# The first three activation blocks of a two-layer decoder trunk, loaded from ScalarE's DMA queue instead of SyncE's

## The chip, the cores and the metric

The kernel runs on one core of one Trainium2 chip. A core has five engines, each with its own instruction stream that is worked off strictly in the order in which it was written into the program: PE (TensorE, matmuls), DVE (VectorE), ACT (ScalarE), POOL (GpSimd) and SP (SyncE, which here only starts DMAs). An engine that meets a wait holds up everything behind it in its own stream. The metric is the device time of one execution in microseconds (us), the median over several runs. Lower is better.

## What is computed

The reference is the forward pass of a decoder trunk of two layers over 256 positions (`S`) of width 2048 (`D`), in float32. Layer 0 mixes dilated sliding-window attention (8 heads) with gated linear attention (GLA, 4 heads); layer 1 mixes an S5 state-space block with HGRN2 heads. Both have one combined input projection, a SiLU gate and one output projection. Cut to what the change touches, which is the very beginning:

```python
def rmsnorm(x, g):
    xf = x.astype(jnp.float32)
    return xf * lax.rsqrt(jnp.mean(xf * xf, axis=-1, keepdims=True) + EPS) * g

def ab_layer(h, w_in, gla_w_gate, gla_b_gate, gla_norm_g, w_out):
    z = h @ w_in                               # h: 256 x 2048, the normalised x
    qa, ka, va, qb, kb, vb, g_low, gate = jnp.split(z, AB_SPLIT, axis=-1)
    ...
    return y @ w_out

h = x
h = h + ab_layer(rmsnorm(h, norm_g[0]), ...)   # layer 0
h = h + cd_layer(rmsnorm(h, norm_g[1]), ...)   # layer 1
out = rmsnorm(h, final_g)
```

## The kernel before

**Tiling.** The activations lie transposed in SBUF: 16 blocks of 128 channels by 256 positions (`kt` = 0 to 15). They share one tile `xv` (L75) with a table of 220 small vectors (`NV`), which stands in its first columns. Every projection is a chain of blocks of 512 output columns. For one block the weights stream in as four groups `g` of four `kt` each, 1 MB a group, into one of three buffers `raw` (L144). A float32 product is built from three products of rounded parts: ACT rounds a weight half group into `wh` (L168), DVE puts what is left into `wl` (L169), and PE adds `wh·xh + wh·xl + wl·xh`, where `xh` and `xl` are the same two parts of the activations, made once by `split_x` (L204 to L206). `gemm_fm` (L174) gives the result with channels on the partitions, 12 matmuls of 256 columns for each `kt` (L181); `gemm_tm` (L193) gives it with positions on the partitions, 6 matmuls of 512 columns for each `kt` (L200). `wh` and `wl` have three buffers each, and one buffer holds two `kt`, so that ACT and DVE can work at most three half groups ahead of PE.

**The first projection.** The very first block (`psq`, L241, the q of GLA) can start only when the first activations and weights have come. For it `load_split` cuts both into smaller pieces. In group 0 each `kt` is loaded alone: first its piece of `xv`, then its weights, and the weights of `kt` 0 in two halves. The piece of `kt` 0 carries the table of vectors with it (476 columns in place of 256). Groups 1 to 3 come in halves of two `kt`. All these loads go through `load` (L229), which starts them on SP's queue and chains each behind the last with `tc.issue_after`, so that SP's order is as written.

**What sets the order.** The program is written with a tile framework that schedules the instructions itself, by a timeline that it estimates while it builds the program (`schedule_with_timeline_sim=True`, L1126). `urgent()` (L72) raises the priority of what stands in it. So the order in which an engine meets its instructions is not that of the source, and an edit at one place can move instructions at others, wherever the estimate of one time tips the choice.

**What comes behind, and is spoken of below.** While the first two projections run, ACT and DVE also square and sum the activations (`square_sum`, L105 to L111, with a single scratch tile `gf`, L109) and DVE works out the S5 parameters (`s5_prep`, L807 to L932, some 150 small operations). When the first projection is done, ACT evacuates it from PSUM into `gq` (L390). The second projection gives k (`gk`, L359), the third and fourth give v by `gemm_tm`. In between PE turns two small S5 matrices `co` round (L937), ACT copies them out (`et`, L938), POOL stores them to DRAM (`ed`, L940) and loads them again spread over the partitions (`E`, L953), and DVE multiplies with them (L976 to L981). GLA's own small matmuls (L287, 32 of 32x32 for each of its levels) are strewn between the projections' matmuls. Much later, around 650 us, ACT sends S5 results `ys` to DRAM (L638), gets them back as `yc` and works on them (L643).

Of the kernel before, what the change touches and what calls it, by code (L numbers as in the profile page):

```python
# [57 lines left out]
def trunk(ctx: ExitStack, tc: tile.TileContext, I, out):  # L58
    nc = tc.nc
# [12 lines left out]
    def urgent():  # L72
        return tc.high_priority(offset=HI)

    xv = const.tile([128, NV + KT * S], F32, name="xv")  # L75
# [59 lines left out]
    def hook():  # L135
        if fillq:
            todo = fillq.pop(0)
            if todo:
                with tc.issue_after(state["mm"].ins):
                    for fn in todo:  # L140
                        fn()

    def load_split(src, g):
        raw = stream.tile([128, 4, 512], F32, name="raw", bufs=3)  # L144
        first = state["first"]
        state["first"] = first and g < 3
        with urgent():
            if first:
                for a, b in ((0, 1), (1, 2), (2, 3), (3, 4)) if g == 0 else ((0, 2), (2, 4)):
                    xs = slice(NV + (4 * g + a) * S if g + a else 0, NV + (4 * g + b) * S)  # L150
                    load(xv[:, xs], I["xv"][:, xs])
                    for c in (slice(0, 256), slice(256, 512)) if g + a == 0 else (slice(0, 512),):
                        load(raw[:, a:b, c], src[g][:, a:b, c])
                for kt in range(4 * g, 4 * g + 4):
                    split_x(kt, V_NG0)
            else:
                state["load"] = nc.sync.dma_start(raw, src[g])
        if first and g == 3:
            load_consts()
        for half in range(2):  # L160
            wh = stream.tile([128, 2, 512], F32R, name="wh", bufs=3)
            wl = stream.tile([128, 2, 512], F32R, name="wl", bufs=3)
            with urgent():
                for a, b, c, d in (((0, 1, 0, 256), (0, 1, 256, 512), (1, 2, 0, 512)) if first and g == 0
                                   else ((0, 2, 0, 512),)):
                    r = raw[:, 2 * half + a:2 * half + b, c:d]
                    w, l = wh[:, a:b, c:d], wl[:, a:b, c:d]
                    state["wh"] = A.activation(w, r, AF.Copy)  # L168
                    V.tensor_sub(l, r, w)  # L169
            for k in range(2):  # L170
                yield 4 * g + 2 * half + k, wh[:, k], wl[:, k]
            hook()
# [13 lines left out]
    def _iter(src, groups, mid, order):  # L186
        for n, g in enumerate(order or range(groups)):
            for m, (kt, wh, wl) in enumerate(load_split(src, g)):
                yield 4 * n + m, kt, wh, wl
            if mid and 2 * (n + 1) == groups:  # L190
                mid()
# [12 lines left out]
    def split_x(kt, go):  # L204
        A.activation(xh[:, kt], hT[:, kt], AF.Copy, scale=col(go + kt))
        V.scalar_tensor_tensor(xl[:, kt], hT[:, kt], col(go + kt), xh[:, kt], op0=OP.mult, op1=OP.subtract)  # L206
# [15 lines left out]
    def load_consts():  # L222
        nc.sync.dma_start(cst, I["cst"])
        nc.sync.dma_start(glw, I["w_low"])
        for n in range(2):
            nc.sync.dma_start(wgt[16 * n:16 * n + 16], I["w_gate"])
        nc.sync.dma_start(msk.rearrange("p a b -> p (a b)"), I["msk"])

    def load(dst, src):  # L229
        prev = state.get("load")  # L230
        with tc.issue_after(prev.ins) if prev else ExitStack():
            state["load"] = nc.sync.dma_start(dst, src)
# [906 lines left out]
```

## Time and profile before

| | us |
|---|---|
| median of 3 runs | 888.54 (887.33 to 891.26) |
| profiled execution, whole | 894.61 |
| its span, first to last instruction | 892.7 |
| DVE busy | 636.0 (71%) |
| ACT busy | 473.1 (53%) |
| POOL busy | 54.4 (6%) |

The profile is of one execution of its own; its 894.61 us lie 6.07 us above the median of the runs, and 1.9 us of it lie outside the span. A row of the timeline reads: start in us, duration in us, engine, source line, operation, tile written `<-` tiles read, form, count, and in brackets the time for which the engine sat idle before it and what ended that. Rows of the same kind are merged, and a duration then runs to the end of the last. Durations of neighbours overlap, since an engine begins an instruction before the last is quite through, so that spacing is read from the starts. `ACTq`, `SPq` rows are the issue of a DMA on that engine's queue. A row of the windows reads: stretch, its length, busy time and instructions of PE, weight load, DVE, ACT and POOL, then the granted clock of PE, the mean busy share of the 16 DMA engines, and GB/s.

### The profile page before, as it was taken

Reading aid. Unit: us, or ns where it says so; the run is one execution under the profiler, and the core shown is the slowest. Engines: PE = TensorE matmul, PEld = TensorE weight load, DVE = VectorE, ACT = ScalarE, POOL = GpSimd, SP = SyncE. Lnnn points to the kernel's source line nnn. Section 1 sums busy time; section 2 is a strip of 40 time slices with the busy share of each in tenths; the row PEclk is TensorE's granted clock in tenths of the full one; section 3 lists DMA queues with packets and bytes.
Section 4 is the critical chain, followed back from the end, with each engine's and each line's share of the span. In section 5 each row is a group of like instructions: output and inputs, shape, how many; then the busy total and the mean of one; then the engine's idle time right before and its main releaser. Section 6 shows DMA issues by size and latency. Waiting matters only on the chain.

```text
span 892.7 us, 18688 instructions
## 1 busy us (share of the span) xinstructions
PE 874.1 (98%) x7728; PEld 804.5 (90%) x7728; DVE 636.0 (71%) x1197; ACT 473.1 (53%) x715; POOL 54.4 (6%) x106
## 2 busy tenths in 40 slices
PE   8999999999999999999999999999999999999995
PEld 8987899888998899999999999899867899988894
DVE  7987975888869868755575586877977655665562
ACT  7654546665655765644443345455545475444451
POOL 0001100111101101000000001100110000000000
PEclk9999999999999999999999999999999999999998
DMA  9827744777756655555575766754654455544432
GB/s 316 318 99 217 257 159 146 231 253 217 264 193 220 223 179 182 206 189 189 190 270 195 267 211 227 247 192 166 222 170 160 183 189 189 189 171 179 176 136 94
DMA packets 40388, 180.40 MB, mean 202 GB/s; under 512 B 12720, under 2 KB 14256, under 8 KB 22768
## 3 DMA queue, kind: packets, MB, share of 16 engines
q1 hardware_dynamic: 29440, 154.99, 49.5%
q0 software_dynamic: 7984, 22.69, 7.7%
q10 hardware_dynamic: 2880, 1.54, 0.6%
q8 instruction: 60, 0.98, 0.4%
q14 instruction: 24, 0.20, 0.1%
HBM read 166.48 MB, written 12.71 MB: 201 GB/s over the span
## 4 chain that ended last, share of the span: by engine, by line
PE 74%; DVE 8%; ACT 6%; DMA 5%; issue 5%; SPq 0%; POOL 0%; POOLq 0%; DVEq 0%; ACTq 0%
PE pg L181 48%; PE pg L200 17%; DVE wl L169 2%; PE pg L758 2%; DMA tabs<-pc 2%; ACT wh L168 1%; PE pm L287 1%; DMA E<-ed 1%; PE pm L339 1%; DMA s5y<-ys 1%; ACT bb L1021 1%; DMA raw<-in_w_dram 1%; ACT x L1039 1%; PE pm L308 1%; DVE PP L1005 1%
## 5 line engine op out<-in xcount | busy, mean ns | idle before, releaser
L168 ACT ACTIVATE wh<-raw 128x1024 fp32r<-128x1024 f32 (+2 forms) x276 | 287.6, 1046 | 325.0 <-PE pg L181 187.6
L169 DVE TENSOR_TENSOR wl<-raw,wh 128x1024 fp32r<-128x1024 f32 (+2 forms) x276 | 332.6, 1207 | 173.7 <-ACT wh L168 165.0
L181 PE MATMUL pg<-xh,wh 128*128 128x256 f32 x1024 | 162.8, 281 | 1.8 <-ACT wh L168 1.7
L181 PE MATMUL pg<-xl,wh 128*128 128x256 f32 x1024 | 163.8, 280 | 0.0
L181 PE MATMUL pg<-xh,wl 128*128 128x256 f32 x1024 | 163.4, 281 | 0.1
L181 PEld LDWEIGHTS pg<-xh,wh 128*128 128x128 f32 x1024 | 137.4, 188 | 3.7 <-ACT wh L168 3.1
L181 PEld LDWEIGHTS pg<-xl,wh 128*128 128x128 f32 x1024 | 138.0, 188 | 0.8 <-issue 0.3
L181 PEld LDWEIGHTS pg<-xh,wl 128*128 128x128 f32 x1024 | 137.9, 189 | 0.8 <-DVE wl L169 0.3
L200 PE MATMUL pg<-wh,xh 128*128 128x512 f32 x320 | 100.4, 395 | 1.8 <-ACT wh L168 1.8
L200 PE MATMUL pg<-wl,xh 128*128 128x512 f32 x320 | 101.0, 396 | 0.5 <-DVE wl L169 0.4
L200 PE MATMUL pg<-wh,xl 128*128 128x512 f32 x320 | 101.0, 395 | 0.0
L200 PEld LDWEIGHTS pg<-wh,xh 128*128 128x128 f32 x320 | 59.3, 188 | 14.8 <-ACT wh L168 2.2
L200 PEld LDWEIGHTS pg<-wl,xh 128*128 128x128 f32 x320 | 59.5, 188 | 14.1 <-DVE wl L169 1.3
L200 PEld LDWEIGHTS pg<-wh,xl 128*128 128x128 f32 x320 | 59.9, 188 | 12.8
L181 PE MATMUL pg<-yh,wh 128*128 128x256 f32 x320 | 50.8, 281 | 0.0
L181 PE MATMUL pg<-yl,wh 128*128 128x256 f32 x320 | 50.6, 281 | 0.0
L181 PE MATMUL pg<-yh,wl 128*128 128x256 f32 x320 | 50.6, 281 | 0.0
L181 PEld LDWEIGHTS pg<-yl,wh 128*128 128x128 f32 x320 | 43.4, 190 | 0.1
L181 PEld LDWEIGHTS pg<-yh,wh 128*128 128x128 f32 x320 | 43.2, 189 | 0.1
L181 PEld LDWEIGHTS pg<-yh,wl 128*128 128x128 f32 x320 | 43.1, 189 | 0.0
L967 POOL DMA_DIRECT2D tabs<-pc x44 | 23.8, 546 | 167.0 <-DVE x L977 43.7
L200 PE MATMUL pg<-wh,yh 128*128 128x512 f32 x96 | 30.1, 394 | 0.0
(350 smaller groups left out, 994.0 us busy)
## 6 DMA issues: line engine op xcount, KB each, us to landing
raw<-in_w_dram SPq DMA_DIRECT2D x100, 1024.0 KB, 5.0
raw<-in_wo_dram SPq DMA_DIRECT2D x28, 1024.0 KB, 4.8
tb<-tabs POOLq DMA_DIRECT2D x8, 768.0 KB, 6.4
tabs<-pc POOLq DMA_DIRECT2D x20, 256.0 KB, 5.7
raw<-in_wg_dram SPq DMA_DIRECT2D x4, 1024.0 KB, 4.8
raw<-in_wo1l_dram SPq DMA_DIRECT2D x4, 1024.0 KB, 4.8
raw<-in_w_dram SPq DMA_DIRECT2D x6, 512.0 KB, 7.4
tabs<-pc POOLq DMA_DIRECT2D x24, 128.0 KB, 4.9
```

Of the source, the lines that this page charges most:

```text
L168: state["wh"] = A.activation(w, r, AF.Copy)
L169: V.tensor_sub(l, r, w)
L181: state["mm"] = T.matmul(ps[:, c], w[:, cs], a[:, kt], start=(i == 0 and n == 0 and c % 2 == 0), stop=(i == last and n == 2), skip_group_c ...
L200: state["mm"] = T.matmul(ps[:, t], a[:, kt, ts_], w, start=(i == 0 and n == 0), stop=(i == last and n == 2), skip_group_check=True)
L287: T.matmul(ps[32 * b:32 * b + 32, t, hd], k[:, hd, r], Q[:, hd, r], start=True, stop=True)
L308: T.matmul(ps[j0:j0 + h, hd, j0 + h:j0 + 2 * h], k[:, hd, b:b + h], Qp[:, hd, b + h:b + 2 * h], start=True, stop=True)
L339: T.matmul(ps[:, (hd - h0) * dv:(hd - h0 + 1) * dv], AT[:, hd, t + j], v[:, j, hd * dv:(hd + 1) * dv], start=(j == 0), stop=(j == t))
L758: T.matmul(ps[:, t, 0:256], a_[:, kt, ts_], w_, start=(kt == 0 and n == 0), stop=(kt == KT - 1 and n == 2), skip_group_check=True)
L967: nc.gpsimd.dma_start(tabs[qt, dst, n], t[src].rearrange("p a b -> p (a b)"))
L1005: V.scalar_tensor_tensor(PP[half[1 - g], g].rearrange("p a b c -> p (a b c)"), x1[half[g]], -1.0, x2[half[g]], op0=OP.mult, op1=OP.subtract)
L1021: A.activation(bb[half[g ^ n], g], z[n][half[g]].unsqueeze(2).to_broadcast([64, 8, 4, 16]), AF.Copy)
L1039: A.activation(v8(x1)[:, r_], cst[:, C_ID64:C_ID64 + 64], AF.Copy, scale=vec[:, V_D + 8 * qt + r_:V_D + 8 * qt + r_ + 1])
```

## The change

```diff
@@ -148,7 +148,10 @@
             if first:
                 for a, b in ((0, 1), (1, 2), (2, 3), (3, 4)) if g == 0 else ((0, 2), (2, 4)):
                     xs = slice(NV + (4 * g + a) * S if g + a else 0, NV + (4 * g + b) * S)
-                    load(xv[:, xs], I["xv"][:, xs])
+                    if g == 0 and a < 3:
+                        nc.scalar.dma_start(xv[:, xs], I["xv"][:, xs])
+                    else:
+                        load(xv[:, xs], I["xv"][:, xs])
                     for c in (slice(0, 256), slice(256, 512)) if g + a == 0 else (slice(0, 512),):
                         load(raw[:, a:b, c], src[g][:, a:b, c])
```

The pieces of `xv` for `kt` 0, 1 and 2 are started on ACT's queue. They stand outside the chain of `load`; the weights stay on SP and stay chained. Nothing else is written differently, but the scheduler gives other orders on PE, DVE, ACT and SP: in the first 120 us of the program, and again at the last S5 quarter around 650 us. In between they agree but for a few DMA issues on SP, and POOL's order is the same throughout. In the listings below the changed kernel's line numbers are 3 higher from L155 on (L171 is L168 of before); the text uses the numbers of before.

The start of ACT's stream before, from its first instruction on (`wact` is a dummy that brings the table load forward, `ge` a small exponential):

```order
L235 ACT_TABLE_LOAD
L235 ACTIVATE wact<-ones 128x1
L205 ACTIVATE xh<-xv 128x256
L168 ACTIVATE wh<-raw 128x256
L258 ACTIVATE ge<-ge 128x16
L168 ACTIVATE wh<-raw 128x256
```

The same place in the changed kernel:

```order
L152 DMA xv<-in_xv_dram 128x476
L152 DMA xv<-in_xv_dram 128x256
L171 ACT_TABLE_LOAD
L171 ACTIVATE wh<-raw 128x256
L152 DMA xv<-in_xv_dram 128x256
L208 ACTIVATE xh<-xv 128x256
L171 ACTIVATE wh<-raw 128x256
```

Two of the loads stand ahead of the table load, the third behind the first rounding of weights, which waits for its data.

ACT at the end of the first projection, before. The first row makes the last `wh` of the first projection, and the two rows of `wh` ahead of `gq` (which evacuates that projection) are the first two of the second projection:

```order
L168 ACTIVATE wh<-raw 128x1024
L107 ACTIVATE sqa<-xv 128x1024
L110 ACTIVATE gf<-xv 128x1024
L368 ACTIVATE glhl<-glw 128x16x16
L110 ACTIVATE gf<-xv 128x1024
L168 ACTIVATE wh<-raw 128x1024 x2
L390 ACTIVATE gq<-pg 128x1024
L110 ACTIVATE gf<-xv 128x1024
L168 ACTIVATE wh<-raw 128x1024 x7
```

The same place in the changed kernel:

```order
L171 ACTIVATE wh<-raw 128x1024
L107 ACTIVATE sqa<-xv 128x1024
L110 ACTIVATE gf<-xv 128x1024
L371 ACTIVATE glhl<-glw 128x16x16
L110 ACTIVATE gf<-xv 128x1024
L393 ACTIVATE gq<-pg 128x1024
L110 ACTIVATE gf<-xv 128x1024
L171 ACTIVATE wh<-raw 128x1024 x8
```

The first two `wh` of the second projection have moved behind the evacuation `gq` and the third squaring `gf`. On DVE the third addition L111 has likewise moved ahead of the second projection's first `wl`.

DVE where the S5 parameters meet their reloaded matrices `E`, before. The `wl` ahead of L976 is the eleventh of the third and fourth projections (v), and the one behind L979 the twelfth:

```order
L169 TENSOR_TENSOR wl<-raw,wh 128x1024
L891 TENSOR_TENSOR up_717<-up_717,tmp 128x32
L976 TENSOR_TENSOR pc<-E,pB 128x512
L977 TENSOR_TENSOR x_1593<-E,pB 128x512
L978 TENSOR_TENSOR pc<-E,pB 128x512
L979 TENSOR_TENSOR x_1594<-E,pB 128x512
L169 TENSOR_TENSOR wl<-raw,wh 128x1024
```

In the changed kernel the `wl` ahead is the fifth of these projections, and the one behind is the sixth:

```order
L172 TENSOR_TENSOR wl<-raw,wh 128x1024
L894 TENSOR_TENSOR up_689<-up_689,tmp 128x32
L330 TENSOR_TENSOR gT_1401<-gT_1363 128x128
L979 TENSOR_TENSOR pc<-E,pB 128x512
L980 TENSOR_TENSOR x_1593<-E,pB 128x512
L981 TENSOR_TENSOR pc<-E,pB 128x512
L982 TENSOR_TENSOR x_1594<-E,pB 128x512
L890 TENSOR_TENSOR tmp<-up_689 128x32
L892 TENSOR_TENSOR up_696<-up_689 128x32
L330 TENSOR_TENSOR gT_1439<-gT_1401 128x64
L172 TENSOR_TENSOR wl<-raw,wh 128x1024
```

The four multiplications that need `E` stand six half groups of weights earlier. What makes `E` has moved as well. PE's two transposes L937 stand before the 53rd and the 61st matmul of v in the old order, and 20 and 11 matmuls before the end of the second projection in the new one; the matmuls L379 that lead to GLA's decay stand 30 matmuls earlier. Of GLA's small matmuls L287, the first two sets of 32 stand in 6 places of PE's old order up to the end of v (5, 1, 4, 3, 2 and 17+32) and in 12 places of the new one.

## The prediction

> **What bounds the kernel now.** I read the page first, then PE's busy time by stretches, then the timeline wherever PE idles or the change moves something.
>
> ```profile
> span 892.7 us, 18688 instructions
> ...
> 0.00:10.00 10.00, 7.72 (x44) 6.85 (x45) 5.20 (x30) 5.71 (x13) 1.76 (x7) 1.00 0.76 225
> ...
> 100.00:150.00 50.00, 48.89 (x731) 45.78 (x730) 35.35 (x57) 27.31 (x51) 2.12 (x4) 1.00 0.54 191
> ...
> 600.00:700.00 100.00, 97.96 (x1162) 84.16 (x1161) 78.36 (x126) 54.23 (x89) 7.38 (x13) 1.00 0.52 180
> ```
>
> PE is the bound. Outside the first 10 us (2.28 us idle), a 1.11 us gap near 117 us and 2.04 us near 650 us it hardly stops before the tail. So what makes PE idle is paid at the end in full, whatever the other engines save.
>
> **The first loads.** Removed from SP: three issues. Added to ACT: three issues, two ahead of the table load, one behind the first `wh`.
>
> ```profile
> 0.73 0.38 SPq L232 DMA_DIRECT2D xv<-in_xv_dram  x1
> 1.17 0.90 SPq L232 DMA_DIRECT2D raw<-in_w_dram  x2
> 0.73 1.28 ACT L235 ACT_TABLE_LOAD   x1 [0.73 <-PEq L1122]
> ...
> 2.00:3.00 1.00, 1.00 (x6) 1.00 (x6) 0.00 (x0) 0.21 (x2) 0.29 (x2) 1.00 0.88 293
> 3.00:4.00 1.00, 1.00 (x7) 1.00 (x5) 0.63 (x8) 0.63 (x2) 0.00 (x0) 1.00 0.66 168
> 4.00:5.00 1.00, 0.81 (x4) 0.34 (x3) 1.00 (x6) 0.38 (x2) 0.00 (x0) 1.00 0.95 296
> 5.00:6.00 1.00, 0.44 (x3) 0.44 (x4) 0.49 (x4) 0.89 (x2) 0.00 (x0) 1.00 0.75 203
> ...
> 12.79 0.73 PE L181 MATMUL pg<-xh,wh 128*128 128x256 f32 x4 [0.53 <-ACT wh L168]
> ```
>
> An issue takes SP about 0.45 us, so the weights can start 0.45 us earlier at once and 1.35 us earlier after the third. But the DMA engines were already 0.88, 0.66, 0.95 and 0.75 busy between 2 and 6 us; what a denser queue can fill there is 0.12 + 0.34 + 0.05 + 0.25 = 0.76 us, and PE's last start-up wait (12.79) hangs on that stream. Against it, ACT issues until 1.65 us and loads its table until 2.93; the first `xv` shares the engines with weights that used to come after it; the third piece waits behind `wh`. I take a gain of 0.6 us (between 1.1 and a loss of 0.5).
>
> The Trainium skill ("DMA: Bandwidth & Descriptors", Issuing engines are not separate DMA queues) says that all queues run on the same 16 engines and a second one saves only issue time; by that rule the gain would be the issue time, up to 1.35 us, and the busy shares above agree that little more than that is there to win. The Trainium skill ("ScalarE: Activation LUTs", What ACT_TABLE_LOAD costs) gives 1.28 us for the load and 1.38 for a drain; by it `wh` would start a little over 1 us later and the gain become a small loss, but the row above is followed by an activation at 2.02, with no drain to be seen.
>
> **Second projection: a new stall.** ACT's stream now has `gq` and the third `gf` ahead of the second projection's first `wh`.
>
> ```profile
> 28.32 1.99 ACT L168 ACTIVATE wh<-raw 128x1024 fp32r<-128x1024 f32 x2
> 30.38 1.03 ACT L390 ACTIVATE gq<-pg 128x1024 f32<-128x1024 f32 x1
> 31.30 1.05 ACT L110 ACTIVATE gf<-xv 128x1024 f32<-128x1024 f32 x1
> 32.25 2.00 ACT L168 ACTIVATE wh<-raw 128x1024 fp32r<-128x1024 f32 x2
> ...
> 29.70 0.64 PE L181 MATMUL pg<-xh,wl 128*128 128x256 f32 x4
> 30.18 0.64 PE L181 MATMUL pg<-xh,wh 128*128 128x256 f32 x4
> ...
> 28.49 1.22 DVE L111 TENSOR_TENSOR sqa<-sqa,gf 128x1024 f32<-128x1024 f32 x1
> 29.90 1.22 DVE L169 TENSOR_TENSOR wl<-raw,wh 128x1024 fp32r<-128x1024 f32 x1
> ```
>
> Before, the first of the two `wh` was ready at about 29.3 and PE went on at 30.18 without a pause. `gq` cannot start until PE's last matmul of the first projection ends (29.70 + 0.64, and it did start at 30.38). In the new order `wh` follows `gq` and `gf`: it takes the place of the row at 32.25, is ready at about 33.3, and PE has nothing to do from 30.18 on: 3.2 us. Then `wl`: DVE must first add the third `gf` (ready 32.35, 1.22 us), so `wl` runs from 33.55 to 34.8, while PE wants it 0.95 us after 33.35: another 0.5. Sum **+3.7 us** (3.2 to 4.3). Nothing covers this; queued behind the waiting `gq` are all further `wh`, and PE waits for those.
>
> **E: the second new stall.** What makes `E` comes earlier, but its reader comes earlier still.
>
> ```profile
> 58.88 0.62 PE L181 MATMUL pg<-xh,wl 128*128 128x256 f32 x4
> 59.33 0.62 PE L200 MATMUL pg<-wh,xh 128*128 128x512 f32 x2
> 59.79 0.62 PE L200 MATMUL pg<-wh,xl 128*128 128x512 f32 x2
> ...
> 62.45 1.06 ACT L385 ACTIVATE gQ<-gQ 128x1024 f32<-128x1024 f32 x1
> 74.35 0.36 ACT L938 ACTIVATE et<-pm 128x256 f32<-128x256 f32 x1
> 79.22 0.63 POOL L953 DMA_DIRECT2D E<-ed  x1 [1.17 <-DMA ed<-et]
> 88.26 0.69 DVE L976 TENSOR_TENSOR pc<-E,pB 128x512 f32<-128x512 f32 x1 [4.08 <-DMA E<-ed]
> 90.68 1.22 DVE L169 TENSOR_TENSOR wl<-raw,wh 128x1024 fp32r<-128x1024 f32 x1
> 91.95 0.73 PE L200 MATMUL pg<-wl,xh 128*128 128x512 f32 x2
> DMA to landing us min/median/max: 6.1/8.4/11.3
> ```
>
> (The last row is that of all eight loads of `E`.) Before, DVE waited 4.08 us for `E`, the `wl` behind it was done at 91.90, and PE took it at 91.95: no slack, and no loss either. I count the new order from T, the first matmul of v (59.33 before). L379 stands 30 matmuls earlier, 30 x 0.118 = 3.5 us, so L385, which ended at T + 4.2, ends at T + 0.7, and `et`, now right behind it and with its transposes long done, at T + 1.1. From the end of `et` to L976 it took 88.26 - 74.71 = 13.55 us: `E` is there at T + 14.65. L976 to L979 and `wl` take 90.68 + 1.22 - 88.26 = 3.64, three small operations between them 0.4: the sixth `wl` is ready at T + 18.7. PE wants it after 60 matmuls of v (0.46 us for two, 13.7), three breaks for L287 (1.5, below) and the four matmuls with `wh` (0.9): T + 16.1. **+2.6 us.** Queued behind the waiting L976 on DVE are all further `wl`, and PE waits for those. With the fastest and the slowest load of `E` in place of the 8.9 us that this one took it would be nothing and 5.0 us; I keep both ends. Afterwards DVE has no more work than before and catches up.
>
> **Breaks on PE.** Small matmuls strewn among large ones cost more than the same in one heap.
>
> ```profile
> 91.10 0.63 PE L200 MATMUL pg<-wh,xl 128*128 128x512 f32 x2
> 91.66 0.27 PE L287 MATMUL pm<-gq,gk 128*32 128x32 f32 x8
> 92.52 0.62 PE L200 MATMUL pg<-wh,xh 128*128 128x512 f32 x2
> ...
> 105.22 0.62 PE L200 MATMUL pg<-wl,xh 128*128 128x512 f32 x2
> 106.77 0.74 PE L181 MATMUL pg<-xh,wh 128*128 128x256 f32 x4
> ```
>
> From 91.10 to 92.52 PE begins two rows of large matmuls (the other is that at 91.95 above) and the small ones between them; 1.42 us pass where two large rows take 0.92: 0.50 for 8 passes. From 105.22 to 106.77 it is 1.55 in place of 0.46: 1.09 for the 98 passes of the 17+32. So a break costs some 0.45, a pass 0.0066. The first two sets have 12 breaks instead of 6: 6 x 0.45 = **+2.7 us** (2.0 to 3.2). They lie on PE itself, nothing covers them.
>
> **What is given back.**
>
> ```profile
> 117.00 0.75 PE L287 MATMUL pm<-gQ,gk 128*32 128x32 f32 x64 [1.11 <-DVE gk L325]
> ...
> 653.88 0.63 ACT L643 ACTIVATE gw<-yc 128x512 f32<-128x512 f32 x1 [6.11 <-DMA yc<-s5y]
> 656.17 0.74 PE L200 MATMUL pg<-wh,xh 128*128 128x512 f32 x2 [1.77 <-ACT wh L168]
> ```
>
> Near 117 us DVE's L325 was late because a `wl` ahead of it waited for ACT, which was busy with S5 copies. These now stand before the end of v, and five `wl` in a row follow: I take the whole 1.1 us back (0 to 1.1). Near 656 us PE waited for a `wh` behind L643, which waited for `yc`. The new order has three `wh` ahead of that L643 in place of two, so 1.8 us go; but in the next piece one send of `ys` stands behind an evacuation and L643 to L647 follow each other with no `wh` between. I take **-1.5 us** (-1.8 to +1.0).
>
> **Sum.** -0.6 + 3.7 + 2.6 + 2.7 - 1.1 - 1.5 = +5.8 us. On the profiled execution (span 892.7, whole 894.61) that is a span of 898.5 and 900.4 in all. That execution lies 6.1 us above the median of the runs; I put the same difference on the median: 888.5 + 5.8 = **894.3 us**, 0.65% slower. One thing stands outside the sum: a row of four L181 matmuls sometimes begins 0.48 after the last (29.70 to 30.18), sometimes 0.45 (58.88 to 59.33). What sets that, the trace does not show; the changed breaks may tip a projection (48 rows) by about a microsecond either way.
>
> **The rivals.**
>
> *E lands in time.* If its load takes under 6.3 us, DVE does not hold up the sixth `wl`. For it: the fastest of eight took 6.1, and this one could meet fewer weights under way, since PE has just stood still. Against it: half of the eight took 8.4 or more. Time: 894.3 - 2.6 = 891.7, within 0.5%.
>
> *The matmul rhythm flips, and the kernel is faster.* Place: the first rows after each break, where the spacing changes between 0.48 and 0.45. Price: 0.02 x 48, about 1 us, for each of the 21 projections of the L181 kind. From six flips to the quicker rhythm the 5.8 us are gone; with eleven it ends at 894.3 - 11 = 883.3. For it: both rhythms are in the trace. Against it: beyond v the order of PE is the old one up to 640 us, so most flips should fall as they did.
>
> *Only the loads count.* The reordering is hidden and what remains is 0.6 to 1.35 us of start: 887.2 to 887.9. Against it: the order puts `wh` behind an evacuation that cannot start early. The rule of the Trainium skill weighed above ("DMA: Bandwidth & Descriptors", Issuing engines are not separate DMA queues) would by itself end here.
>
> **How the numbers follow.** A measurement of this kernel can tell about 0.5% (4.4 us) from no change. Chances: forecast 0.64, E in time 0.20, rhythm 0.11, loads alone 0.05. Of the forecast 0.55 lies above 893.0, since small values of E's wait and a larger gain near 656 us fall below; of "E in time" 0.04 lies above; of the rhythm 0.06 below 884.1. So slower 0.59, within 0.35, faster 0.06. The range goes from 888.0, which takes in E in time and six flips of the rhythm, to 899.5, where E's slowest load (+2.4) and the lost gain at 656 us (+2.5) add to the sum.
>
> **What would show it.** Right: PE idle 3 to 4 us at the end of the first projection, ended by ACT's `wh`; DVE idle some 4 to 5 us before L976 and PE idle about 3 us behind it, before its 65th matmul of v; twelve groups of L287 within v; no idle at the later 117 us place; less at 656 us; the wait at 12.79 a little earlier. Wrong: no gap at the first evacuation, or PE's time lost in places that I have not named.

## The result and the profile after

The changed kernel took 903.5 us (median of four runs, 901.38 to 904.68), the kernel before 888.12 in the same series. The ratio is 1.0166, with a 95% interval of 1.0143 to 1.0189: slower by 15 us, not by 6. The profiled execution took 902.34.

The page's first line and the stretches of PE that the prediction used, with two that turned out to matter (busy time of PE, its weight loads, DVE, ACT, POOL, then the granted PE clock, the DMA share and GB/s):

```profile
span 900.5 us, 18682 instructions
```

```profile
0.00:10.00 10.00, 8.09 (x39) 7.55 (x40) 4.00 (x24) 4.70 (x11) 1.76 (x7) 1.00 0.78 225
30.00:40.00 10.00, 7.00 (x36) 6.80 (x36) 8.34 (x25) 5.86 (x6) 0.00 (x0) 0.66 0.49 179
80.00:90.00 10.00, 4.30 (x29) 3.13 (x28) 6.77 (x14) 1.02 (x1) 1.15 (x2) 0.69 0.23 70
100.00:150.00 50.00, 50.00 (x637) 43.64 (x636) 33.73 (x61) 25.90 (x41) 2.14 (x4) 1.00 0.57 206
600.00:700.00 100.00, 98.08 (x1250) 85.54 (x1237) 79.76 (x130) 52.73 (x86) 7.37 (x13) 1.00 0.49 169
```

The idle near 117 us is gone, as forecast; near 650 us nothing was won. The new thing is a column, not a gap: the clock, 1.00 in all of the rows shown of before, is 0.66 and 0.69 in two stretches.

The first is the new stall behind the first projection. ACT and PE there:

```profile
30.36 1.02 ACT L393 ACTIVATE gq<-pg 128x1024 f32<-128x1024 f32 x1 [2.15 <-PE pg L184]
31.29 1.05 ACT L110 ACTIVATE gf<-xv 128x1024 f32<-128x1024 f32 x1
32.23 1.05 ACT L171 ACTIVATE wh<-raw 128x1024 fp32r<-128x1024 f32 x1
```

```profile
29.71 0.62 PE L184 MATMUL pg<-xh,wl 128*128 128x256 f32 x4
33.33 1.22 PE L184 MATMUL pg<-xh,wh 128*128 128x256 f32 x4 [3.00 <-ACT wh L171]
34.35 1.05 PE L184 MATMUL pg<-xl,wh 128*128 128x256 f32 x4
35.20 1.05 PE L184 MATMUL pg<-xh,wl 128*128 128x256 f32 x4
```

The wait is the one forecast, ended by the `wh` forecast. But the rows after it begin 0.85 us apart in place of 0.45. PE and its clock by single microseconds:

```profile
32.00:33.00 1.00, 0.00 (x0) 0.77 0.49 205
33.00:34.00 1.00, 0.67 (x3) 0.50 0.08 33
38.00:39.00 1.00, 1.00 (x6) 0.50 0.55 180
39.00:40.00 1.00, 1.00 (x9) 0.82 1.02 434
40.00:41.00 1.00, 1.00 (x11) 1.00 0.80 336
```

If the clock is either at 1.00 or at 0.50, as the rows around say, 0.77 means that it fell at 32.54, and 0.82 that it rose at 39.36. From 33.33 to 39.36 PE worked at half rate: half of 6.03 us, 3.0 us, are lost on top of the 3.0 us of waiting.

The second stretch is `E`: its issue on POOL and what the tile's view says of its two loads, its reader on DVE with the `wl` behind it, and PE:

```profile
71.51 1.26 POOL L956 DMA_DIRECT2D E<-ed  x2 [3.65 <-DMA ed<-et]
```

```profile
DMA to landing us min/median/max: 6.8/8.9/11.0
```

```profile
83.23 0.69 DVE L979 TENSOR_TENSOR pc<-E,pB 128x512 f32<-128x512 f32 x1 [8.76 <-issue]
...
85.99 1.22 DVE L172 TENSOR_TENSOR wl<-raw,wh 128x1024 fp32r<-128x1024 f32 x1
```

```profile
65.56 0.62 PE L203 MATMUL pg<-wh,xh 128*128 128x512 f32 x2
...
87.26 1.22 PE L203 MATMUL pg<-wl,xh 128*128 128x512 f32 x2 [5.70 <-DVE wl L172]
88.28 1.05 PE L203 MATMUL pg<-wh,xh 128*128 128x512 f32 x2
...
122.03 0.73 PE L184 MATMUL pg<-xh,wh 128*128 128x256 f32 x4
```

DVE waited 8.76 us for `E` (its row names only "issue", but the second load, issued at 72.1, landed 11.0 us later) and PE 5.70 for the `wl` behind it, at the 65th matmul of v as forecast; then rows of two 0.86 apart in place of 0.46. The first row is the first matmul of v (59.33 before), the last the end of v (106.77 before): 6.2 us late at the one, 15.3 at the other.

### The profile page after: what moved, and what is told of

It is laid out like the page before. It is cut to its first block, busy times and chain, and to the rows that moved or that the text cites. A ratio compares the mean times of both kernels' runs of the same rounds, so it can differ in the third digit from the quotient of the medians.

```text
span 900.5 us, 18682 instructions
## 1 busy us (share of the span) xinstructions
PE 876.1 (97%) x7728; PEld 804.3 (89%) x7728; DVE 636.2 (71%) x1197; ACT 472.4 (52%) x715; POOL 54.4 (6%) x106
## 4 chain that ended last, share of the span: by engine, by line
PE 80%; DMA 7%; DVE 5%; ACT 4%; issue 3%; ACTq 0%; POOLq 0%; SPq 0%; POOL 0%; DVEq 0%
PE pg L184 48%; PE pg L203 23%; DMA s5y<-ys 2%; PE pg L761 2%; DMA yc<-s5y 2%; DVE wl L172 1%; PE pm L342 1%; PE pm L290 1%; ACT wh L171 1%; DMA raw<-in_w_dram 1%; DMA E<-ed 1%; PE pm L311 1%; PE pm L418 1%; DMA ed<-et 1%; PE pm L1030 1%
## 5 line engine op out<-in xcount | busy, mean ns | idle before, releaser
L171 ACT ACTIVATE wh<-raw 128x1024 fp32r<-128x1024 f32 (+2 forms) x276 | 287.6, 1046 | 337.5 <-PE pg L184 195.6
```

## Experiments

The theory was that the order makes the loss, each stall priced at its idle time plus a spell of halved clock, and that the loads themselves are nearly free. The rival was that issuing the loads from ScalarE's queue costs the time. Line numbers in rows of experiments are those of the kernel named and lie a few lines off.

### The order without the loads, with a flaw

The loads stay on SyncE. The second projection's first `wh` is held behind `gq` and the third `gf`, and the rest of the new order follows from that by itself:

```
-        A.activation(q, psq, AF.Copy, scale=128 ** -0.5)
+        state["gate"] = A.activation(q, psq, AF.Copy, scale=128 ** -0.5)
...
+                    with ExitStack() as st:
+                        for gate in ("gate", "gf") if state.get("gate") else ():
+                            st.enter_context(tc.issue_after(state[gate].ins))
+                        state["wh"] = A.activation(w, r, AF.Copy)
```

> The loads stay on SyncE's queue; only the order of ScalarE is made that of the changed kernel at one place (the evacuation gq and the third gf stand ahead of the second projection's first wh), from which nearly the whole order of the changed kernel follows, the twelve breaks on PE and the early read of E among them. Theory (the new order costs the time, the loads themselves nothing): 903 us, ratio to the kernel before 1.013 to 1.020; PE waits about 3.0 us for wh near 30 us and 4 to 6 us for wl near 85 us, and behind each the granted clock is 0.50 for some 6 us; the first projection's last start-up wait stands at 12.8 us as before. Rival (the loads on ScalarE's queue cost the time, by their late issue and by what they push back): 887 to 891 us, with PE's waits near 30 and 85 us under 1 us or without loss.

923.87 us, ratio 1.0378 (1.0345 to 1.0410). Both stalls are there (3.00 and 5.22 us), but 20 us too much: the gate was never cleared, so later projections' `wh` were held behind the next norm's square as well. PE's rows behind those three added waits:

```profile
422.44 1.22 PE L184 MATMUL pg<-yh,wh 128*128 128x256 f32 x4 [4.41 <-ACT wh L171]
...
450.43 1.22 PE L184 MATMUL pg<-yh,wh 128*128 128x256 f32 x4 [4.41 <-ACT wh L171]
...
479.69 0.74 PE L184 MATMUL pg<-xh,wh 128*128 128x256 f32 x4 [4.41 <-ACT wh L171]
```

By accident this is a good measurement. PE and its clock around the first two of these waits:

```profile
422.00:423.00 1.00, 0.56 (x2) 0.66 0.00 0
425.00:426.00 1.00, 1.00 (x7) 0.63 0.10 25
449.00:450.00 1.00, 0.00 (x0) 0.81 0.00 0
456.00:457.00 1.00, 1.00 (x9) 0.77 0.97 410
```

Read as before, the same wait of 4.41 us three times lowered the clock three times, but for 3.4 us (422.3 to 425.7, and 480.3 to 483.8 behind the third) or for 6.8 (449.6 to 456.5), and once only after PE was already working again.

### The order without the loads, mended

As above, with one line more, so that only one `wh` is held:

```
+                    state["gate"] = None
```

> The run of the order alone, mended: in that kernel the first wh of every later projection was also held behind a norm's square, and its trace shows three waits of PE of 4.41 us near 422, 450 and 480 us that the changed kernel does not have. Now only the second projection's first wh is held. The three waits (13.2 us) and the halved clock behind them (3.4, 6.8 and 3.4 us at 0.50) go, about 20 us in all. Theory (the order costs the time, the loads about 1 us of start): 902 to 905 us, ratio 1.013 to 1.018; first matmul of v at 64.4 us, end of v at 121 us. Rival (something else in that run was slow): over 910 us.

902.32 us, ratio 1.0141 (1.0103 to 1.0179), v begins at 64.12: the theory's case. PE's two waits:

```profile
33.10 1.22 PE L185 MATMUL pg<-xh,wh 128*128 128x256 f32 x4 [3.00 <-ACT wh L171]
...
83.39 0.74 PE L204 MATMUL pg<-wl,xh 128*128 128x512 f32 x2 [3.27 <-DVE wl L173]
```

Without a single load moved, nearly all of the loss is there. The end of v (118.22) missed its 121 us, because `E`'s loads took 6.4 and 8.7 us this time, and PE's wait for it was 3.27 us: how long `E` travels differs from one profile to the next, and what makes it differ was not tried.

### The loads without the order

The loads as changed; `gq` and the third `gf` held behind the second `wh`, the products of `E` behind the 31st `wl` (`whs` and `wls` list these instructions in order; the constraints set the order of issue on an engine and add no wait):

```
+    def evac_q():
+        with tc.issue_after(whs[13]), urgent():
+            state["gq"] = A.activation(q, psq, AF.Copy, scale=128 ** -0.5)
+        tc.add_manual_dep(state["gf"].ins, state["gq"].ins.name, mybir.DependencyInfo(
+            mybir.DependencyClass.NoSync, mybir.DependencyReason.DATA), reason="order")
+    fillq.extend([[], [evac_q]])
...
+            with tc.issue_after(state["wls"][30]) if qt == 0 else ExitStack():
                 cmul2(w2, (E[:, :, 0], E[:, :, 1]), (Bt[:, 0], Bt[:, 1]), v8(x1), v8(x2))
```

> The three loads are issued by ScalarE as in the changed kernel, but gq and the third gf are held behind the second projection's second wh and the products of E behind the 31st wl, where the kernel before had them. Theory: 886 to 891 us, ratio 0.998 to 1.003; the last start-up wait stands 0.6 us later than before (13.4 us), no wait of PE over 2 us afterwards, and the granted clock is 1.00 from 10 us to the tail. Rival (the loads cost the time): 897 us or more, ratio over 1.010.

892.83 us, ratio 1.0039 (1.0018 to 1.0061): far from the rival's 897, but above the theory's 886 to 891. Its profiled execution spans 885.8 us; no wait of PE after 10 us is over 1.1 us and the clock stays at 1.00. So it was timed again beside the kernel before as a null run.

> The kernel before, unchanged, timed as the changed ones were. Theory (a ratio of 1.004 is a real difference): 0.998 to 1.002. Rival (a kernel measured this way comes out 0.2 to 0.4% over the kernel before whatever is in it, as the five kernels without a long wait did, at 1.0026 to 1.0064): 1.002 or more.

> The run with the loads alone, timed again beside the null run, because its trace (v begins and ends 0.6 and 0.8 us later than in the second look at the kernel before, both spans 886 us) shows less than the 3.5 us of its ratio 1.0039. Theory (the loads by themselves cost at most the 1 us that the trace shows; the rest is the spacing of the matmul rows, which differs from one execution to the next): ratio 0.999 to 1.003, within 0.2% of the null run. Rival (the loads cost 3 us that lie where the one trace does not show them): 1.003 to 1.006, over the null run by 0.3% or more.

The null run gave 888.56 us, 1.0006 (0.9992 to 1.0019), the loads alone 891.79 us, 1.0022 (0.9999 to 1.0046). These two do not separate at 95%, but both timings of the loads lie over 1. By the traces this kernel ends v 0.8 to 1.9 us later (108.12 and 108.45, against 107.34 and 106.55 in two further profiles of the kernel before). The loads alone need not be the cause of all of it, since the pinned order is not quite that of before: small S5 operations stand ahead of a `wl` on DVE, so that PE waits 1.10 and 0.46 us for it near 32 us (0.56, 0.32 and nothing in the three profiles of before), and v is broken in nine places, not seven. More of the 0.2 to 0.4% changes from one execution to the next in one place: between 620 and 720 us the two profiles of this one kernel differ.

The first profile's stretch:

```profile
620.00:720.00 100.00, 98.75 (x1060) 82.02 (x1059) 75.15 (x119) 54.36 (x88) 7.38 (x13) 1.00 0.53 183
```

The second profile's:

```profile
620.00:720.00 100.00, 96.06 (x1034) 78.94 (x1033) 75.09 (x115) 51.59 (x77) 6.78 (x12) 1.00 0.50 175
```

### Only the first piece from ScalarE

As the loads without the order, with `a < 1` in place of `a < 3`.

> As the run with the loads alone (order of the kernel before at gq and at E), but only the first piece of xv is issued by ScalarE, the second and third by SyncE again. Theory (what the loads cost at the start, 1.0 us at the first matmul of v, comes from the second issue ahead of the table load and from the third, which waits on ScalarE behind the first wh and lands at 8.8 us): v begins at 59.0 to 59.8 us, 886 to 890 us, ratio 0.997 to 1.001. Rival (a first load from ScalarE's queue is late by itself): v at 60.3 us or later, 891 us or more.

892.21 us, ratio 1.0037 (1.0009 to 1.0065), v at 61.77: the rival's numbers. The theory's explanation of the start fails, since with one piece it is no better than with three; that a first load from ScalarE is late by itself is not shown by one profile either. PE's last start-up wait came at 14.67 here, while kernels with all loads on SyncE showed 12.79 to 13.49 and kernels with three on ScalarE 13.14 to 13.65. What sets this within a microsecond or two stays open.

### Each stall undone alone

First `gq` alone (its part of the diff above):

> As the changed kernel, but gq and the third gf are held behind the second projection's second wh, as before; E is still read early (behind the 28th wl, before it was the 31st, in the changed kernel the 25th). Theory (each stall costs its own length and as much again in halved clock: 3.0 + 2.7 us at gq; 5.7 + 1.5 us at E): the gq part goes whole, and of E's wait 0 to 2.5 us stay, since E is wanted three wl later and made about 4 us later: 889 to 894 us, ratio 1.001 to 1.007. Rival (a stall costs its idle time alone, and E's wait does not hang on where E is read): 903.5 - 3.0 = 900 us.

> The kernel in which gq and the third gf are held back and E is read behind the 28th wl, looked at again, because its first profiled execution was disturbed throughout. Theory: no wait for wh near 30 us over 1 us; before the projection v's matmul that needs the 29th wl PE waits 1 to 3 us for E's reader, and if that is over 2 us the clock is halved for 3.4 us or more behind it; end of v at 109 to 113 us. Rival (what 895.8 us hold against 892.8 of the run with E late too is spread): no wait near 85 us, end of v at 108 to 109 us.

The median of six executions is 895.28 us (a seventh, at 2190.79, is left out), ratio 1.0063 (1.0041 to 1.0086): the ratio is the theory's, the time a little over its 889 to 894. The second profile shows no wait near 30 us over 0.8 us, and none for `E`'s reader at all, so nothing is left there of the wait that the theory expected; by the waits it is the second rival's case, though v ends at 109.38 and not at 108 to 109. That profile also gives the price of the breaks by itself: small matmuls break v in twelve places, as in the changed kernel, PE waits for nothing in it, and v takes 48.80 us against 47.34 to 47.59 in the kernel before with seven breaks. So five more cost 1.2 to 1.5 us. What its span of 891.4 us has over the 885.8 of the loads alone lies in part near 650 us again (PE is busy 96.13 of 100 us between 620 and 720). Then `E` alone (its part of the diff above):

> As the changed kernel, but the products of E are held behind the 31st wl, where the kernel before had them; gq still stands ahead of the second projection's first wh. Theory: the wait of 5.7 us for wl and the 1.5 us of halved clock behind it go, the wait of 3.0 us for wh near 30 us and its halved clock (0.50 from 33 to 39 us) stay: 903.5 - 7.2 = 896.3 us (894 to 898.5), ratio 1.009. Rival (idle time alone counts): 903.5 - 5.7 = 897.8 us with no more than what the wait held; or E's late read turns into another wait behind the end of v, and the time stays over 900 us.

895.42 us, ratio 1.0064 (1.0043 to 1.0086): forecast 896.3. PE's wait near 85 us is gone, and v takes 47.46 us, as before. The pin undoes the breaks too (v has seven here), so the 8 us won are `E` and breaks together. The 3.00 us wait near 30 us is still there, but this time the clock fell only 1.4 us after PE had gone on, and for 3.4 us (35.1 to 38.5).

```profile
65.20 0.62 PE L205 MATMUL pg<-wh,xh 128*128 128x512 f32 x2
...
112.66 0.74 PE L186 MATMUL pg<-xh,wh 128*128 128x256 f32 x4
```

### Is it PE's idling that halves the clock?

As the run with `E` undone, with 11 matmuls of a constant on PE behind the first projection, whose result nobody reads:

```
     psq = gemm_fm(w0[0], 4, xh, xl)
+    fill(11)
```

> As the run with E's late read (gq still ahead of the second projection's first wh, PE waits 3.0 us near 30 us), but 11 matmuls of ones with ones, whose result nobody reads, stand on PE behind the first projection's last matmul and fill the wait. Theory (the halved clock comes from PE's idle time): the wait for wh ends when it did, the clock stays 1.00, the rows behind it are 0.455 us apart and the first matmul of v comes 1.5 to 3.1 us earlier, at 62.1 to 63.7 us (65.20 without the fill); 892 to 894 us. Rival (the clock falls for another reason, the stop of the DMA stream or the evacuation): the rows stay 0.855 apart for 3.4 us or more, v begins at 65 us or later, 895 us or more.

PE with the fill (the trace counts two passes for each of the 11 matmuls):

```profile
30.36 2.62 PE L148 MATMUL pm<-ones 128*128 128x128 f32 x22
33.53 0.74 PE L196 MATMUL pg<-xh,wh 128*128 128x256 f32 x4 [0.55 <-ACT wh L181]
34.10 0.63 PE L196 MATMUL pg<-xl,wh 128*128 128x256 f32 x4
```

`wh` comes no earlier, but the clock stays 1.00, and v begins at 63.44 in place of 65.20. That is 1.8 us, against a spell of 3.4 us at half rate in the kernel without the fill, worth 1.7. So it is PE's idling that halves the clock. The whole, 894.81 us (1.0064, 1.0031 to 1.0097), lies between the theory's and the rival's and does not resolve it.

### How long a wait may be

The loads on SyncE, `E` read late, and only `gq` ahead of the `wh`:

> The kernel before (loads on SyncE) with gq alone ahead of the second projection's first wh, the third gf behind it, and E read behind the 31st wl as before: PE's wait near 30 us is about 2.0 us in place of 3.0. Theory (a wait of 2 us is too short to lower the clock, as the 1.8 us before were): clock 1.00, v begins at 59.3 + 2.0 = 61.4 us, 891 to 893 us, ratio 1.001 to 1.004. Rival (any wait of about 2 us halves the clock for 3.4 us or more): v at 63 us or later, 893.5 us or more.

893.40 us, ratio 1.0035 (1.0009 to 1.0061). The theory's threshold was wrong; PE waits 2.06 us, works a microsecond at full rate, and then the clock falls:

```profile
32.20 0.74 PE L184 MATMUL pg<-xh,wh 128*128 128x256 f32 x4 [2.06 <-ACT wh L170]
32.77 0.67 PE L184 MATMUL pg<-xl,wh 128*128 128x256 f32 x4
33.46 1.22 PE L184 MATMUL pg<-xh,wl 128*128 128x256 f32 x4
```

v begins at 63.20, as the rival has it; the whole lies between the two cases. Then the same with half of `gq`:

```
-        state["gate"] = A.activation(q, psq, AF.Copy, scale=128 ** -0.5)
+        state["gate"] = A.activation(q[:, 0:2], psq[:, 0:2], AF.Copy, scale=128 ** -0.5)
```

> As the run with the short wait (loads on SyncE, E read late), but only the first half of gq stands ahead of the second projection's first wh, the other half behind the second wh: PE's wait there is about 1.55 us in place of 2.06. Theory (the clock is lowered at the end of a stretch of 3.4 us in which PE idled for more than about half; 1.55 us is too little wherever the stretch falls): clock 1.00 throughout, v begins near 61.0 us (63.20 less 0.5 of the wait and 1.7 of the halved clock), 890 to 892 us. Rival (any wait over about 1 us lowers it when it falls badly): 0.50 for 3.4 us, v at 62.5 us or later.

```profile
32.31 0.74 PE L184 MATMUL pg<-xh,wh 128*128 128x256 f32 x4 [1.63 <-ACT wh L170]
32.88 0.62 PE L184 MATMUL pg<-xl,wh 128*128 128x256 f32 x4
```

The clock stays 1.00 and v begins at 61.65, between the two cases; the whole took 892.13 us (1.0026, 1.0002 to 1.0050), just above the theory's 890 to 892. Between these two kernels 0.43 us of waiting make 1.55 us at the start of v.

### The kernel before, profiled again

The two profiled executions differ by 7.8 us in span, the medians by 15.4, and beyond v the changed kernel was 7.5 us quicker.

> The kernel before, unchanged, looked at a second time. From the end of v on, its first profiled execution took 751.8 us to the tail's first projection, the changed kernel's 744.3, with rows of four yh matmuls 0.470 us apart there and 0.450 here. Theory (the spacing is a matter of the execution, and the 7.5 us are nothing that the change gives back): this time most rows are 0.450 apart, that stretch takes 743 to 748 us, and the whole 886 to 890 us. Rival (the order of the kernel before is slower there, and the change gives 7.5 us back): 751 to 752 us again, with 0.470.

887.74 us, span 885.9. The groups of `yh` rows, first profile and second:

```profile
L181 PE MATMUL pg<-yh,wh 128*128 128x256 f32 x320 | 50.8, 281 | 0.0
```

```profile
L181 PE MATMUL pg<-yh,wh 128*128 128x256 f32 x320 | 49.6, 276 | 0.0
```

From the end of v to the tail it took 744.40 us this time (107.34 to 851.74), the changed kernel 744.30. Nothing comes back: the first profile had many rows 0.47 apart, this one and that of the changed kernel mostly 0.45. Of the 7.4 us between the two profiles of the kernel before, 2.4 are idle time of PE, and the rest, some 5, goes with that spacing. So the second one is what to set beside the profile after: 900.5 - 885.9 = 14.6 us.

## Why the prediction was wrong

Measured against that second profile (v begins at 59.75 and ends at 107.34), the steps come out so.

- **PE is the bound, and what makes it idle is paid in full.** Right.
- **The first loads, -0.6.** Wrong in sign, small in size: the last start-up wait ended at 13.37 in place of 12.79, and the first projection's last row begins at 29.71 in place of 29.14 (in the first profile of before, with its slower rows, at 29.70). The third piece did wait behind `wh`, was issued at 4.32 and landed at 9.0; but with the first piece alone on ScalarE the start was no better, so which part of the change costs the 0.6 us stays open.
- **Second projection, +3.7.** The mechanism and the wait were right (3.00 us). The step that failed is "PE has nothing to do: 3.2 us", which prices a stall at its idle time. With the halved clock it came to 3.0 + 3.0 us, and v began 5.8 us late. (The 0.6 us of the first loads are in that too; but the second profile of before had lost 0.56 us to a `wl` at 31.4, which the changed kernel did not.) The 0.5 us that the forecast had for `wl` disappeared in the slow rows.
- **`E`, +2.6.** Place, reader and matmul were right. `et` was done at T + 0.4, earlier than forecast, but from there to L979 it took 17.2 us and not 13.55; the wait was 5.70 us, just beyond the 5.0 that the slowest load gave. Half rate from 87.26 to 90.56 adds 1.6. Together 7.3 us; in the mended run of the order alone, with quicker loads, the wait was 3.27.
- **Breaks of L287, +2.7.** v took 56.5 us in place of 47.6; less 7.3 for `E` that leaves 1.6, and the run without the waits has 1.2 to 1.5 for the same. Both the count and the price were too high: one of the two transposes L937 had broken v by itself and now stands ahead of it, so that v has five breaks more and not six, and from 71.51 to 72.88 a break of 12 passes costs 0.45 us, where the prediction's prices give 0.53.
- **Given back at 117 us, -1.1.** Right: from the end of v to the first 512-column row near 630 us (626.92 before, 640.45 changed) the changed kernel is 1.2 us quicker; 0.9 of it is the wait at that place.
- **Near 656 us, -1.5.** Wrong: the stretch behind is 1.1 us slower. The wait for `wh` went, three others (0.98, 0.44 and 0.36 us) came. Since one and the same kernel, the loads alone, lost 1.3 us there in one profile and 3.9 in another, no small term could be forecast here from a single trace.

Sum: 5.8 + 7.3 + 1.6 - 1.2 + 1.1 = 14.6 us. Of the 8.8 us that the forecast of 5.8 lacks, 4.6 are the halved clock, which no term of it held, 3.1 are `E`'s longer way and 2.6 the place near 656 us; the breaks, priced too high, take 1.1 back.

Two sums of the prediction are off by little and change nothing: 30 rows of 0.46 are 13.8 and not 13.7, and 894.3 + 2.4 + 2.5 is 899.2 and not 899.5.

**The rivals.** `E` did not land in time. The rhythm of the rows is real, and it moved the first profile of the kernel before by some 5 us, but both spacings are seen in one and the same kernel. "Only the loads count" fell with the mended run of the order: the order alone gives a ratio of 1.0141, the whole change 1.0166. That the profiled execution's 6.1 us over the median were put on both sides was right; they were mostly that rhythm.

**The missing row.** The trace of before showed waits of PE of at most 1.77 us with the clock at 1.00, and nothing longer outside the start. A 3 us wait was therefore something that the trace did not show, and its price should have had an upper end. The Trainium skill ("TensorE: Matmul & The Clock Gate", What's actually happening) has the rule that was missing: the clock is at half after an idle window of about 3.4 us and full again after a busy one, in windows that run freely. The lengths agree (3.4 us, or two of them), but by the letter of that rule the 3.00 us wait would have left the clock alone; the last section has what these traces show in its place.

## What to carry to other kernels

A wait on the engine that bounds the kernel does not cost its length alone: from 2.06 us on it also bought 3.4 or 6.8 us of half rate here, so price it both ways, and shorten it or fill it where it can't be removed. Moving a DMA issue to another engine's queue in a program whose order is computed changes that order far from the edit; compare the two orders, and pin with an order constraint the two or three places on which the bounding engine waits. And before two traces are compared stretch by stretch, profile one of the kernels twice: here two profiles of the kernel before differ by 6.8 us.

No kernel here beat the one before: the loads alone, its best form, is equal to it or 2 to 3.5 us slower.

## What the runs showed of the hardware

- The clock changes on a grid of its own. Read as above, in the run with the flaw it fell at 33.20, 84.40, 422.32, 449.62 and 480.34 us and rose at 36.62, 91.22, 425.74, 456.46 and 483.76: all of these lie whole multiples of 3.4133 us apart, within 0.02 us, and so do the changes in each other trace, with a phase of its own. Since in every trace the clock falls once more after the last matmul, that phase is known for the kernel before and for the shorter waits too. Cut along it, the 14 undisturbed traces agree behind the first 9 us: the clock fell at the end of every full-rate stretch in which PE had been idle for 0.60 of it or more, and of none with 0.53 or less; it rose after stretches with 0.07 or less of idling, and stayed low after those with 0.23 or more. So a wait is priced by how much of it falls into one stretch, and the fall can come a microsecond after work has begun again (the 2.06 us wait).
- Waits of PE of 1.63, 1.72 and 1.77 us left the clock at 1.00; 2.06, 3.00, 3.27, 4.41, 5.22 and 5.70 us halved it. A spell that began 0.8 us or more before work did lasted two stretches, since the first of them still held 0.23 or more of idling; those that began 0.3 us or less before it, or after it, lasted one. The Trainium skill ("TensorE: Matmul & The Clock Gate", Why this matters for your kernels) advises against gaps of PE over about 3 us; here 2.06 us was already too long.
- At the start the clock column can't be trusted: it reads 1.00 while rows of four lie 0.85 us apart (6.45 to 7.30 in the changed kernel, 6.13 to 6.99 in the null run), as they do at 0.50. PE begins at half rate (14 passes of 128 columns take 3.32 us from 0.99 on, where 22 such passes of the fill take 2.62), and its rows lie 0.45 apart from 8.85 us on in the changed kernel, from 9.59 in the null run and by 5.91 in the first profile of before.
- Rows of four matmuls of 256 columns are 0.45 or 0.47 us apart at a granted clock of 1.00, over whole projections, and the same kernel showed both. What sets it stays open; it makes some 5 us of the difference between the two profiles of the kernel before.
- One kind of load of 256 KB, the two of `E`, took 5.7 to 14.1 us from issue to landing where these kernels load it first. What makes one slow was not tried.
